# Turning the sample's queries and keys to features over the whole TensorE array, in a hybrid decoder step

## The chip, the cores and the metric

The kernel runs on one core of a Trainium2 chip. The metric is the time of one execution on the device, in microseconds; the median of several runs is taken. The profile is of one execution. Its engines are PE (TensorE: matmuls and transposes), PEld (TensorE's load of the stationary operand), DVE (VectorE), ACT (ScalarE), POOL (GpSimd), and SP, which issues DMAs here.

## The reference, cut to what matters

One inference step of a decoder trunk of two layers, for a prompt of 512 tokens and for a sample group of 8 x 4 = 32 tokens that share all weights. Each layer projects the normalized tokens to ten pieces, mixes them in three groups of heads, and projects back:

```
rq, rk, rv, rg, mq, mk, mv, mg, pu, pg = jnp.split(rmsnorm(x) @ w_in, _split_points(), axis=-1)
# A: retention, 6 heads of 64      (rope; state carried; group norm)
# B: block-sparse attention, 6 heads of 64 (queries and keys normed and roped)
# C: causal pooling over windows 2/4/8/16
mix = concat(r_o * silu(rg), m_o * silu(mg), p_o * silu(pg))
y = x + mix @ w_out
```

The sample's attention reads 2048 earlier positions per sequence through a page table (8 blocks of 256, the best three of them and the own tokens); its retention starts from a given state. Everything is float32. Projections of the prompt are made in three passes of split operands (`F32R`).

## The kernel before, in words

**Tiles.** Tokens lie in 4 tiles of 128 prompt rows and a fifth with the 32 sample rows. A projected query or key tile has tokens on the partitions and 384 features (6 heads of 64) along them. To take scores, it must have features on the partitions, so it is turned by TensorE: three transposes (`tr`, line 360) of 128 features each, against the identity, into a PSUM tile of the ring `tr` (two buffers). For the sample's 32 rows this is done by two functions: `to_blocks` (line 756) for queries, which copies the result to the block layout `qblk` (attention) or a `tabs` buffer (retention), in six small copies, and `to_feat` (line 708) for keys, which copies it to `kTs` in one. In both, a transpose of 32 rows takes a strip of 32 array rows; the kernel calls the mode `ROWS32`. Each is called for two tiles in a layer: eight groups of three transposes in all, 12 of `qk` buffers (queries) and 12 of `ks` buffers (keys).

**Buffers.** A sample's query tile uses one of the three `qk` buffers, a sample's key tile the one `ks` buffer, each 128 x 384; only the first 32 rows are written for the sample. The `qk` buffers serve prompt tiles and residuals in between.

**Modes of the array.** Most matmuls use the whole array (`FULL`). Decode scores and values (`dec`, `pv` in 128x32 forms) divide it by columns, attention values and retention scores in other ways. The planner counts a cost for each change.

**Order.** The order of all instructions on PE, ACT, DVE and POOL is written out by a planner, `_Plan` (line 111 on), when the program is built. Every piece of work is a generator that asks for an engine, keys, buffers and a mode with `R(...)`; the planner starts whichever piece can start first by its estimated times, and adds up an engine's estimated time as instructions are written (`use`, `array`). In `_start`, a piece for PE that isn't of the dense projections counts as due some time after it is ready: `MARGIN` 0.4 us in the undivided mode, `HOLD` 0.6 us if it changes the array away from it, 0.3 or 0.2 us in the other cases. A change of mode costs 0.1 us in the plan, and a transpose 0.06 us for up to 32 rows or 0.1095 us. Work marked "DVE|POOL", as the subtraction for the low half of a weight (`whl`), goes to POOL where DVE's queue is more than 3 us longer. All DMAs of the stretch are issued from SP in the planner's order.

**Start.** `clear` (line 1798) sets constants on POOL, among them `qblk` and `klz`; the first instructions of VectorE turn the first tokens into `XT` (a scaled copy, then a subtraction), and split the first weights (`whl`).

Of the kernel before, what the change touches and what calls it, by code (L numbers as in the profile page):

```python
# [20 lines left out]
NS = 32  # L21
NTOK = SEQ + NS
NB = 8
# [96 lines left out]
class _Plan:  # L120
# [66 lines left out]
        return self.dma_free + 2.8  # L187

    def _start(self, t):
        engines, keys, get, mode = t["want"]  # L190
        at = t["ready"]
        if engines == t.get("engine"):
            at -= self.HOP[engines]
        for k in keys:
            if k not in self.done:
                return None
            at = max(at, self.done[k])
        for name in set(get):
            n = get.count(name)
            r = self.res[name]  # L200
            if len(r) < n:
                return None
            at = max(at, sorted(r)[n - 1])
        best = None
        for e in engines.split("|"):
            s = max(at, self.free[e])
            if e == "SP":
                s = max(s, self.dma_free - 3.0)
            c = s + (self.POOL_LAST if e == "POOL" and "|" in engines else 0.0)
            if e == "PE" and t["prio"][0] < 9:  # L210
                late = self.MARGIN
                if mode != self.mode:
                    late = self.HOLD if self.mode == FULL else 0.3
                elif mode != FULL:
                    late = self.STAY
                c = max(at + late, self.free[e])
            elif e == "PE" and self.mode != FULL:
                c = s + self.LEAVE
            if best is None or c < best[0]:
                best = (c, s, e)  # L220
        c, s, e = best
        return c if e == "PE" else s, s, e
# [30 lines left out]
FULL, COLS32, COLS64, ROWS64, ROWS32 = (128, 128), (128, 32), (128, 64), (64, 128), (32, 128)  # L253


def R(engines, keys=(), get=(), mode=FULL):
    return engines, tuple(keys), tuple(get), mode


class _Timed:  # L260
# [58 lines left out]
def trunk(ctx, tc, depth, xp, xt, xs, xst, kv, sret, spool, pt, nrow, ncol, lpar, w384, w256, cst, y0,  # L319
# [3 lines left out]
    X = _Plan()  # L323
# [23 lines left out]
    def tiles(n):  # L347
        return 32 if n <= 32 else 64 if n <= 64 else 128
# [11 lines left out]
    def tr(out, in_, n):  # L360
        nc.tensor.transpose(out, in_, ident[:n, :n])  # L361
        X.array((tiles(n), 128), 0.1095 if n > 32 else 0.06)
# [344 lines left out]

    def to_feat(src, dst, rows, keys=()):

        yield R("PE", keys, ["tr"], (tiles(rows), 128))  # L710
        p = ps("tr")
        for i in range(3):
            tr(p[:, i * rows:(i + 1) * rows], src[:, i * 128:(i + 1) * 128], rows)
        yield R("ACT|DVE")
        copy(dst(), p[:, :3 * rows].rearrange("p (k n) -> p k n", k=3))
        X.put("tr")

    def feat_tile(L, name, tag, src, t):
# [36 lines left out]

    def to_blocks(src, dst):

        yield R("PE", (), ["tr"], ROWS32)
        p = ps("tr")
        for i in range(3):  # L760
            tr(p[:, i * NS:(i + 1) * NS], src[:, i * 128:(i + 1) * 128], NS)
        yield R("ACT|DVE")
        for i in range(3):
            for h2 in range(2):
                hs = slice(64 * h2, 64 * h2 + 64)
                c0 = (2 * i + h2) * 4
                copy(dst[hs, i, :, c0:c0 + 4], p[hs, i * NS:(i + 1) * NS].rearrange("p (b q) -> p b q", b=NB))
        X.put("tr")

    def head_pick(pv_, out):  # L770
# [43 lines left out]
    def layer(l):  # L814
        ci = l * len(order)
        L = {}
# [172 lines left out]
        def post_mq(t):  # L989
            def f(a):  # L990
                yield R("DVE", [("tabs", l, 0)], ["qk"])
                q_ = buf("qk")
                yield from projected(a, q_, t, L["tabs", 0][:, 0, t], L["tabs", 0][:, 1, t], eps=eps_of(t), norm=norm)
                L["roped", 0] = L.get(("roped", 0), 0) + 1
                if L["roped", 0] == 5:
                    X.put("tabs")
                if t < 4:
                    yield from stacked_tile(L, "qT", q_, t)
                    X.put("qk")
                    X.flag("qT", l, t)  # L1000
                else:
                    L["own"] = [sb([128, HD], "own", 2) for _ in range(2)]
                    L["stat"] = [sb([128, 4, 9], "stat", 2) for _ in range(2)]
                    yield from to_blocks(q_[:NS], qblk)
                    X.put("qk")
                    X.flag("qblk", l)
                    for g in range(2):
                        for n in range(BLOCKS):
                            X.spawn(unit(g, n), 2)
                        X.spawn(combine(g), 1)  # L1010
            return f
# [50 lines left out]
        def post_mk(t):  # L1062
            def f(a):
                tag = "qk" if t < 4 else "ks"
                yield R("DVE", [("tabs", l, 1)], [tag])
                k_ = buf(tag)
                rows = 128 if t < 4 else NS
                yield from projected(a, k_, t, L["tabs", 1][:, 0, t], L["tabs", 1][:, 1, t], eps=eps_of(t), norm=norm)
                L["roped", 1] = L.get(("roped", 1), 0) + 1
                if L["roped", 1] == 5:  # L1070
                    X.put("tabs")
                if t < 4:
                    yield from stacked_tile(L, "kT", k_, t)
                    X.flag("kT", l, t)
                    send(o_kp[l, t * 128:(t + 1) * 128], k_, 196, (), "qk")
                    if t == 0:
                        for qi in range(4):
                            for i in range(3):
                                X.spawn(attention(qi, i), 2)
                else:  # L1080
                    yield R("PE", (), ["kTs"])
                    L["kTs"] = buf("kTs").rearrange("p (i n) -> p i n", i=3)
                    yield from to_feat(k_[:NS], lambda: L["kTs"], NS)
                    X.flag("kTs", l)
                    send(o_ks[l], k_[:NS], 48, (), "ks")
                    X.spawn(own_units(), 1)
            return f
# [190 lines left out]
        def post_rq(t):  # L1278
            def f(a):
                yield R("DVE", (), ["qk"])  # L1280
                q_ = buf("qk")
                rows = 128 if t < 4 else NS
                yield from projected(a, q_, t, cos[:, t], sin[:, t], False if t < 4 else rqs[:rows, t], norm=norm)
                if t < 4:
                    yield from feat_tile(L, "rqT", "qT", q_, t)
                    X.flag("rqT", l, t)
                else:
                    yield R("POOL", (), ["tabs"])
                    rqblk = buf("tabs")
                    G.memset(rqblk, 0.0)  # L1290
                    L["rqblk"] = rqblk.rearrange("p (i b c) -> p i b c", i=3, b=NB)
                    yield from to_blocks(q_[:NS], L["rqblk"])
                    X.flag("rqs", l)
                X.put("qk")
            return f
# [21 lines left out]
        def post_rk(t):  # L1317
            def f(a):
                if t == 0:
                    X.spawn(load_state(), 4)  # L1320
                tag = "qk" if t < 4 else "ks"
                yield R("DVE", (), [tag])
                k_ = buf(tag)
                rows = 128 if t < 4 else NS
                yield from projected(a, k_, t, cos[:, t], sin[:, t], rks[:rows, t] if l or t == 4 else rks0[:, t],
                                     norm=norm)
                if t < 4:
                    yield from feat_tile(L, "rkT", "kT", k_, t)
                    X.spawn(ret_state(t, k_), 0)
                    X.spawn(ret_chunk(t), 2)  # L1330
                else:
                    yield R("PE", (), ["kTs"])
                    L["rkTs"] = buf("kTs").rearrange("p (i n) -> p i n", i=3)
                    yield from to_feat(k_[:NS], lambda: L["rkTs"], NS)
                    X.spawn(ret_sample(), 0)
                    yield R("ACT", (), ["kst"])
                    L["kst"] = buf("kst")
                    yield from stacked(k_[:NS, :384], L["kst"], 2)
                    X.put("ks")
                    X.flag("kst", l)  # L1340
            return f
# [456 lines left out]
    def clear():  # L1798
# [9 lines left out]
        for h2 in range(2):  # L1808
            G.memset(klz[64 - 64 * h2:128 - 64 * h2, h2::2, :].bitcast(F32), 0.0)

    def warm(n):

        yield R("PE", [("ones",)], ["att", "att"])
        o_ = ps("att")[:, 0]
        for _ in range(n):
            mm(o_[:, :128], ones, ones)
            X.use("PE", 0.2)
        X.put("att", 2)
# [96 lines left out]
```

## Time and profile before

| | us |
|---|---|
| median of 3 runs (lowest to highest) | 690.66 (689.52 to 691.14) |
| the profiled execution: its time | 690.34 |
| its span, first to last instruction | 688.6 |
| PE busy in it | 674.9 (98%) |
| DVE busy | 490.4 (71%) |
| ACT busy | 329.8 (48%) |
| POOL busy | 96.9 (14%) |

The span is what the rows of the trace cover; the time has some 1.7 us around it. A matmul's row overlaps the next one's, so PE's busy time is not its work at full rate. The chain of waits follows the work that ended last back to the start, and gives each piece the time from the end of the piece before it to its own end.

### The profile page before, as it was taken

Reading aid. Unit: us, or ns where it says so; the run is one execution under the profiler, and the core shown is the slowest. Engines: PE = TensorE matmul, PEld = TensorE weight load, DVE = VectorE, ACT = ScalarE, POOL = GpSimd, SP = SyncE. Lnnn points to the kernel's source line nnn. Section 1 sums busy time; section 2 is a strip of 40 time slices with the busy share of each in tenths; the row PEclk is TensorE's granted clock in tenths of the full one; section 3 lists DMA queues with packets and bytes.
Section 4 is the critical chain, followed back from the end, with each engine's and each line's share of the span. In section 5 each row is a group of like instructions: output and inputs, shape, how many; then the busy total and the mean of one; then the engine's idle time right before and its main releaser. Section 6 shows DMA issues by size and latency. Waiting matters only on the chain.

```text
span 688.6 us, 17002 instructions
## 1 busy us (share of the span) xinstructions
PE 674.9 (98%) x5958; PEld 570.9 (83%) x5958; DVE 490.4 (71%) x1181; ACT 329.8 (48%) x835; POOL 96.9 (14%) x129
## 2 busy tenths in 40 slices
PE   9998999999999999999999999999999999999997
PEld 8876887777877887999999887877787878889897
DVE  6988887787664469984684789987576545888651
ACT  7562757673342424274464347766432332336620
POOL 2252223000000012300112222230000000132000
PEclk9999999999999999999999999999999999999999
DMA  9947889798989974425744779889979989520462
GB/s 316 323 151 241 272 283 290 248 313 262 313 270 327 321 257 148 127 77 192 242 160 135 226 231 297 262 282 286 307 212 320 308 272 330 181 64 1 135 225 73
DMA packets 111382, 159.76 MB, mean 232 GB/s; under 512 B 13953, under 2 KB 96130, under 8 KB 111298
## 3 DMA queue, kind: packets, MB, share of 16 engines
q1 hardware_dynamic: 110866, 158.42, 71.3%
q8 instruction: 47, 0.77, 0.5%
q10 hardware_dynamic: 432, 0.27, 0.2%
q14 instruction: 37, 0.30, 0.1%
HBM read 148.80 MB, written 9.84 MB: 230 GB/s over the span
## 4 chain that ended last, share of the span: by engine, by line
PE 79%; DVE 13%; POOL 2%; issue 2%; DMA 2%; ACT 2%; ACTq 0%; DVEq 0%; SPq 0%; POOLq 0%
PE acc L351 50%; PE dec L351 10%; PE pv L351 10%; PE tr L361 6%; PE att L351 4%; DVE whl L313 2%; DVE qk L313 1%; POOL gst L313 1%; DVE t L313 1%; POOL qst L313 1%; DVE qT L313 1%; ACT PT L313 1%; DVE bns L313 1%; DMA qk<-y 1%; DVE row L313 1%
## 5 line engine op out<-in xcount | busy, mean ns | idle before, releaser
L351 PE MATMUL acc<-whl,XT 128*128 128x384 f32 (+1 forms) x1680 | 310.6, 337 | 0.8 <-DVE whl L313 0.8
L351 PEld LDWEIGHTS acc<-whl,XT 128*128 128x128 f32 x1680 | 281.0, 189 | 18.4 <-issue 13.5
L351 PE MATMUL acc<-XT,whl 128*128 128x256 f32 (+1 forms) x960 | 138.0, 295 | 1.7 <-DVE qk L313 1.2
L351 PEld LDWEIGHTS acc<-XT,whl 128*128 128x128 f32 x960 | 124.6, 189 | 7.8 <-issue 4.1
L313 DVE TENSOR_TENSOR whl<-wraw,whl 128x768 fp32r<-128x768 f32 (+1 forms) x96 | 87.3, 920 | 13.9 <-ACT whl L313 13.1
L313 ACT CAST whl<-wraw 128x768 fp32r<-128x768 f32 (+1 forms) x100 | 76.5, 783 | 28.9 <-PE acc L351 22.7
L351 PE MATMUL dec<-pk,qblk 128*32 128x256 f32 x768 | 48.1, 383 | 0.0
L313 DVE TENSOR_TENSOR pv<-pv,cst 128x384 f32<-128x384 f32 x40 | 22.4, 561 | 25.2 <-PE pv L351 25.0
L351 PEld LDWEIGHTS dec<-pk,qblk 128*32 128x32 f32 x768 | 22.0, 109 | 17.8 <-issue 4.1
L313 DVE TENSOR_TENSOR mix<-acc,qk 128x384 f32<-128x384 f32 (+1 forms) x24 | 12.3, 511 | 22.9 <-PE acc L351 21.9
L313 ACT ACTIVATE P<-att,ast 128x128 f32<-128x128 f32 (+3 forms) x48 | 25.2, 529 | 6.8 <-DVE ast L313 6.2
L313 POOL TENSOR_TENSOR qst<-qst,mhalf 128x6 f32<-128x6 f32 (+1 forms) x20 | 26.5, 1325 | 1.7
L313 ACT ACTIVATE dPT<-dec 128x256 f32<-128x256 f32 x32 | 12.2, 382 | 29.1 <-PE pv L351 28.9
L313 ACT ACTIVATE t<-acc 128x256 f32<-128x256 f32 (+1 forms) x32 | 12.7, 396 | 27.3 <-PE acc L351 16.1
L313 ACT ACTIVATE dP<-dec,stat 128x256 f32<-128x256 f32 x32 | 15.2, 474 | 20.7 <-DVE stat L313 20.6
L313 POOL TENSOR_SCALAR gst<-gst 128x6 f32<-128x6 f32 (+1 forms) x12 | 4.0, 337 | 137.3 <-DVE gst L313 125.2
L361 PE MATMUL tr<-cst,qk 128*128 128x128 f32 (+1 forms) x108 | 18.4, 280 | 4.7 <-DVE qk L313 4.6
L313 ACT ACTIVATE PT<-PT,gst 128x64 f32<-128x64 f32 x48 | 16.8, 429 | 10.2 <-POOL gst L313 10.2
L361 PEld LDWEIGHTS tr<-cst,qk 128*128 128x128 f32 (+1 forms) x108 | 12.3, 142 | 11.2 <-DVE qk L313 4.7
L313 DVE TENSOR_TENSOR t<-acc,cst 128x192 f32<-128x192 f32 x32 | 9.9, 351 | 16.1 <-PE acc L351 16.1
L313 DVE TENSOR_REDUCE ast<-att 128x2 f32<-128x256 f32 (+3 forms) x24 | 19.8, 825 | 0.8
L313 POOL TENSOR_TENSOR gst<-gst,reps 128x6 f32<-128x6 f32 x4 | 0.9, 221 | 137.1 <-DVE gst L313 137.1
(505 smaller groups left out, 1202.8 us busy)
## 6 DMA issues: line engine op xcount, KB each, us to landing
pk<-kv SPq DMA_DIRECT2D x256, 192.0 KB, 3.8
wraw<-w SPq DMA_DIRECT2D x76, 384.0 KB, 5.2
wraw<-w SPq DMA_DIRECT2D x24, 256.0 KB, 4.1
y<-mix SPq DMA_DIRECT2D x4, 512.0 KB, 3.5
mix<-xt SPq DMA_DIRECT2D x7, 256.0 KB, 5.4
pk<-w SPq DMA_DIRECT2D x4, 384.0 KB, 5.4
o_vp<-tv SPq DMA_DIRECT2D x8, 192.0 KB, 2.3
o_kp<-qk SPq DMA_DIRECT2D x8, 192.0 KB, 4.6
```

Of the source, the lines that this page charges most:

```text
L313: return f(*args, **kw)
L351: nc.tensor.matmul(out, lhsT, rhs, start=start, stop=stop)
L361: nc.tensor.transpose(out, in_, ident[:n, :n])
```

## The change

The three transposes of a sample tile take all 128 rows of its buffer and the whole identity, in mode `FULL`, and write 128 columns each of the PSUM tile; the copies behind them pick the first 32 columns of each 128. So that the rows that no sample token fills hold numbers from the start, `clear` sets the three `qk` buffers and the `ks` buffer to zero on POOL, as its last step, and a key `cleared` is asked for by the transposes in the plan. `R` gets a further argument, `hold`, which `_start` would use in place of `HOLD`. `to_feat` serves the prompt's retention tiles too, with 128 rows; for them nothing but the key is new.

```diff
--- before.py
+++ after.py
@@ -187,7 +187,7 @@
         return self.dma_free + 2.8
 
     def _start(self, t):
-        engines, keys, get, mode = t["want"]
+        engines, keys, get, mode, hold = t["want"]
         at = t["ready"]
         if engines == t.get("engine"):
             at -= self.HOP[engines]
@@ -210,7 +210,7 @@
             if e == "PE" and t["prio"][0] < 9:
                 late = self.MARGIN
                 if mode != self.mode:
-                    late = self.HOLD if self.mode == FULL else 0.3
+                    late = (hold or self.HOLD) if self.mode == FULL else 0.3
                 elif mode != FULL:
                     late = self.STAY
                 c = max(at + late, self.free[e])
@@ -253,8 +253,8 @@
 FULL, COLS32, COLS64, ROWS64, ROWS32 = (128, 128), (128, 32), (128, 64), (64, 128), (32, 128)
 
 
-def R(engines, keys=(), get=(), mode=FULL):
-    return engines, tuple(keys), tuple(get), mode
+def R(engines, keys=(), get=(), mode=FULL, hold=None):
+    return engines, tuple(keys), tuple(get), mode, hold
 
 
 class _Timed:
@@ -707,12 +707,13 @@
 
     def to_feat(src, dst, rows, keys=()):
 
-        yield R("PE", keys, ["tr"], (tiles(rows), 128))
+
+        yield R("PE", [("cleared",), *keys], ["tr"])
         p = ps("tr")
         for i in range(3):
-            tr(p[:, i * rows:(i + 1) * rows], src[:, i * 128:(i + 1) * 128], rows)
+            tr(p[:, i * 128:(i + 1) * 128], src[:, i * 128:(i + 1) * 128], 128)
         yield R("ACT|DVE")
-        copy(dst(), p[:, :3 * rows].rearrange("p (k n) -> p k n", k=3))
+        copy(dst(), p[:, :384].rearrange("p (k n) -> p k n", k=3)[:, :, :rows])
         X.put("tr")
 
     def feat_tile(L, name, tag, src, t):
@@ -755,16 +756,16 @@
 
     def to_blocks(src, dst):
 
-        yield R("PE", (), ["tr"], ROWS32)
+        yield R("PE", [("cleared",)], ["tr"])
         p = ps("tr")
         for i in range(3):
-            tr(p[:, i * NS:(i + 1) * NS], src[:, i * 128:(i + 1) * 128], NS)
+            tr(p[:, i * 128:(i + 1) * 128], src[:, i * 128:(i + 1) * 128], 128)
         yield R("ACT|DVE")
         for i in range(3):
             for h2 in range(2):
                 hs = slice(64 * h2, 64 * h2 + 64)
                 c0 = (2 * i + h2) * 4
-                copy(dst[hs, i, :, c0:c0 + 4], p[hs, i * NS:(i + 1) * NS].rearrange("p (b q) -> p b q", b=NB))
+                copy(dst[hs, i, :, c0:c0 + 4], p[hs, i * 128:i * 128 + NS].rearrange("p (b q) -> p b q", b=NB))
         X.put("tr")
 
     def head_pick(pv_, out):
@@ -1001,7 +1002,7 @@
                 else:
                     L["own"] = [sb([128, HD], "own", 2) for _ in range(2)]
                     L["stat"] = [sb([128, 4, 9], "stat", 2) for _ in range(2)]
-                    yield from to_blocks(q_[:NS], qblk)
+                    yield from to_blocks(q_, qblk)
                     X.put("qk")
                     X.flag("qblk", l)
                     for g in range(2):
@@ -1080,7 +1081,7 @@
                 else:
                     yield R("PE", (), ["kTs"])
                     L["kTs"] = buf("kTs").rearrange("p (i n) -> p i n", i=3)
-                    yield from to_feat(k_[:NS], lambda: L["kTs"], NS)
+                    yield from to_feat(k_, lambda: L["kTs"], NS)
                     X.flag("kTs", l)
                     send(o_ks[l], k_[:NS], 48, (), "ks")
                     X.spawn(own_units(), 1)
@@ -1289,7 +1290,7 @@
                     rqblk = buf("tabs")
                     G.memset(rqblk, 0.0)
                     L["rqblk"] = rqblk.rearrange("p (i b c) -> p i b c", i=3, b=NB)
-                    yield from to_blocks(q_[:NS], L["rqblk"])
+                    yield from to_blocks(q_, L["rqblk"])
                     X.flag("rqs", l)
                 X.put("qk")
             return f
@@ -1331,7 +1332,7 @@
                 else:
                     yield R("PE", (), ["kTs"])
                     L["rkTs"] = buf("kTs").rearrange("p (i n) -> p i n", i=3)
-                    yield from to_feat(k_[:NS], lambda: L["rkTs"], NS)
+                    yield from to_feat(k_, lambda: L["rkTs"], NS)
                     X.spawn(ret_sample(), 0)
                     yield R("ACT", (), ["kst"])
                     L["kst"] = buf("kst")
@@ -1808,6 +1809,12 @@
         for h2 in range(2):
             G.memset(klz[64 - 64 * h2:128 - 64 * h2, h2::2, :].bitcast(F32), 0.0)
 
+        yield R("POOL", (), ["ks"] + ["qk"] * RES["qk"])
+        for tag in ["ks"] + ["qk"] * RES["qk"]:
+            G.memset(buf(tag), 0.0)
+            X.put(tag)
+        X.flag("cleared")
+
     def warm(n):
 
         yield R("PE", [("ones",)], ["att", "att"])
```

## Rows read from the trace of the kernel before

**Rows 1.** The page's fourth part: shares of the chain that ended last.
```profile
PE 79%; DVE 13%; POOL 2%; issue 2%; DMA 2%; ACT 2%; ACTq 0%; DVEq 0%; SPq 0%; POOLq 0%
```

**Rows 2.** Chain of waits, first 30 us (start, us, what); shares of 29 to 45 us.
```profile
5.94 0.42 DVE XT L313 x2
...
8.00 7.27 PE acc L351 x40
...
by line: POOL qst L313 39.6%; DVE qk L313 12.2%; issue 9.6%; DVE qT L313 9.6%; DVE t L313 7.3%; DVE qst L313 5.9%; POOL rs L313 5.5%; DVE kT L313 4.8%; DVE acc L313 3.5%; DVE stat L313 2.6%; DVE psc L313 1.5%; DVE rs L313 1.1%; DVE gnw L313
```

**Rows 3.** Chain of waits, 50 to 63 us; last row PE's timeline with its wait.
```profile
50.20 2.51 DVE whl L313
...
58.76 4.33 PE acc L351 x18
...
57.86 0.90 PE L361 MATMUL tr<-cst,qk 128*128 128x128 f32 x3 [2.40 <-DVE qk L313]
```

**Rows 4.** Instructions of line 361: ns minimum, median, maximum; first and last start; forms.
```profile
L361 PE MATMUL tr<-cst,qk x108: 221/272/476, 37.6 to 604.6; 128*128 128x128 f32 x96, 32*128 32x32 f32 x12
...
L361 PE MATMUL tr<-cst,ks x12: 221/222/246, 77.3 to 564.0; 32*128 32x32 f32 x12
```

**Rows 5.** Chain of waits at three groups of narrow transposes.
```profile
157.80 0.89 PE tr L361 x7
...
375.81 0.30 PE tr L361 x3
376.10 2.30 PE acc L351 x12
...
509.85 1.80 PE acc L351 x12
```

**Rows 6.** Chain of waits at undivided transposes and the work beside them.
```profile
402.19 0.48 PE tr L361 x3
...
407.64 3.17 PE acc L351 x18
410.81 0.33 PE tr L361 x3
...
411.14 2.11 PE acc L351 x12
...
438.77 1.59 PE acc L351 x12
```

**Rows 7.** Timeline of POOL at the start (start, us, instruction, idle before).
```profile
1.59 0.77 POOL L313 MEMSET Sst<- 128x384 f32 x2
2.42 2.80 POOL L313 MEMSET klz<- 64x1536 f32 x2
20.04 1.17 POOL L313 TENSOR_TENSOR rs<-rs,mhalf 128x1 f32<-128x1 f32 x1 [14.82 <-DVE rs L313]
```

**Rows 8.** Timeline of VectorE at the start.
```profile
4.86 0.51 DVE L313 TENSOR_SCALAR XT<-mix,ncol 128x256 fp32r<-128x256 f32 x1 [4.86 <-DMA ncol<-ncol]
5.94 0.35 DVE L313 TENSOR_SCALAR XT<-mix,ncol 128x256 fp32r<-128x256 f32 x1 [0.57 <-DMA mix<-xt]
```

**Rows 9.** Timelines of VectorE and POOL, 48 to 52 us and 112 to 115 us.
```profile
48.78 0.96 DVE L313 TENSOR_TENSOR whl<-wraw,whl 128x768 fp32r<-128x768 f32 x1
...
50.12 2.59 DVE L313 TENSOR_TENSOR whl<-wraw,whl 128x768 fp32r<-128x768 f32 x1
...
49.90 1.99 POOL L313 TENSOR_TENSOR whl<-wraw,whl 128x768 fp32r<-128x768 f32 x1 [1.12 <-ACT whl L313]
...
112.95 0.72 DVE L313 TENSOR_SCALAR P<-P,ast 128x256 f32<-128x256 f32 x1
...
112.20 1.31 POOL L313 TENSOR_TENSOR s<-tabs 128x676 f32<-128x676 f32 x1
113.59 1.31 POOL L313 TENSOR_TENSOR tabs<-s 128x672 f32<-128x672 f32 x1
```

**Rows 10.** Table of stretches: busy time of engines, granted clock, DMA share, GB/s.
```profile
58.00:60.00 2.00, 2.00 (x8) 2.00 (x9) 1.24 (x4) 1.17 (x3) 0.00 (x0) 0.50 0.86 267
```

## Prediction

> **What bounds the kernel now.** I read the page's head first. The profiled execution took 690.34 us with a span of 688.6 us; the runs' median is 690.66, so what is summed against the profiled execution gets 0.32 us added at the end. The chain of work that ended last is 79% TensorE and 13% VectorE [rows 1]. An average hides stages, so I read the chain in order of time next. Its start belongs to VectorE: the token load lands, VectorE makes `XT` of it from 5.94 us, and its subtraction for `whl` releases TensorE at 8.00 [rows 2]. From about 22 to 91 us the chain belongs mostly to VectorE, and to the roots on POOL that VectorE waits for: the shares of the stretch from 29 to 45 us show what that looks like, with no TensorE piece among them [rows 2]. In that stretch TensorE waits 2.40 us in one piece, behind a VectorE subtraction that took 2.59 us [rows 3, 9]. From 91 us on the chain is nearly all TensorE. So a microsecond saved on TensorE counts after 91 us, and one lost on VectorE counts before.
>
> **The transposes.** There are 12 narrow transposes of `qk` tiles and 12 of `ks` tiles, 32x128 in and 32x32 of identity [rows 4]: eight groups of three. What one group costs in its place is read from the chain of waits, where a piece lasts from one end to the next. Between undivided work the narrow group takes 0.30 us and the 12 matmuls behind it 2.30 [rows 5]; three undivided transposes take 0.33 and the same 12 matmuls, with the same follower, 2.11 [rows 6]. So the transposes themselves get 0.03 dearer, and the return to the undivided array, 0.19, goes: 0.16 us saved.
>
> Now the eight places, each as it stands today:
> - 37.64 and 77.28 us, where both sorts begin [rows 4]: in the VectorE stretch, off the chain. Saved 0.16 each, worth nothing; the cover is the wait at 57.86 and the VectorE chain to 91 us.
> - 375.81 [rows 5], and 220.47 and 415.94 which are like it (undivided work on both sides): 0.16 each, together -0.48.
> - 509.55 comes right behind decode matmuls, which leave the array divided anyway. Today 0.30, as at 375.81, and 1.80 for the 12 matmuls behind [rows 5]; an undivided group behind divided work takes 0.48, and 12 matmuls of that form 1.59 [rows 6]: 2.10 against 2.07, -0.03. At 157.80, also behind decode work, seven transposes take 0.89 together [rows 5]; undivided 0.48 + 4 x 0.11 = 0.92 (0.11 is a third of 0.33): +0.03.
> - 563.91 is followed by divided work, so the change of mode only comes later and no return is saved: 0.33 for 0.30, +0.03.
>
> The sum is -0.45 us. The bounds: all six on the chain at 0.19 give -1.14; if no place saves anything and each pays 0.03, +0.18. I keep -0.45 because each place has its own rows. Copies out of PSUM keep their number and elements, only strided: nothing in the rows prices a stride, and two of the eight groups lie off the chain; their readers (`qblk`, `kTs`, the table) begin decode units, for which TensorE has other work at all six places, so I take zero.
>
> A page of the Trainium skill speaks against the change. The row first: a narrow group takes 0.30 and an undivided one 0.33 [rows 5, 6], though the identity that it goes through has 128 columns and not 32 [rows 4]. If time went by columns, an undivided group would take 4 x 0.30 = 1.20, and six on the chain 6 x 0.90 = 5.4 us more. The skill's "TensorEngine Tiling (Array Packing)", sections "Theoretical Speedup" and "Tiling Modes", gives up to 4x for a dimension of 32 or less, and a drain at each change of mode; by its factor, too, the sum would be about +5.4 instead of -0.45. The rows bear out the drain and not the factor.
>
> **The memsets.** Four memsets of 128x384 join POOL's queue at the end of `clear`. Two of that size took 0.77 us together today [rows 7], so four take about 1.55 us, and they follow `klz`, which ends at 2.42 + 2.80 = 5.22: they run from about 5.2 to 6.8. On POOL nothing is queued behind them until 20.04 [rows 7], and the cleared buffers are first wanted by the joins of the sample's projections, ahead of the first transpose at 37.64 [rows 4]: the decode and dense work between covers them. No DMA is moved and SP's queue is untouched. But VectorE is working then, on the chain [rows 2]. Its first `XT` instruction, while `klz` is being cleared, took 0.51 us and ended at 5.37, 0.15 behind the memset; the second took 0.35 with POOL idle [rows 8]. The same pattern stands later: a VectorE scaling issued at 112.95 took 0.72 and ended 0.16 after POOL's instruction of 112.20 + 1.31, and POOL's next one at 113.59 didn't keep it out [rows 9]. So the second `XT` instruction, at 5.94, falls among the memsets and may wait for one of them to end: nothing if it falls between two, at most one memset, 0.39, since it gets in before the next. The two-input instructions behind it might wait for another 0.39: no row shows one beside a memset. Bounds 0 to 0.8; I take 0.2, the middle of the first wait alone. It goes in full down the chain: `whl`, the start of TensorE at 8.00 and all behind it.
>
> The skill's "SBUF — State Buffer", section on the two physically separate sides, says why: the port pair of VectorE and GpSimd is an exclusive lock, but an instruction with two SBUF inputs meets it only against a GpSimd instruction that reads SBUF, which a memset doesn't. By that the upper end would be 0.4, not 0.8; no row before the change shows it.
>
> **The order.** `_Plan` writes out the whole order from estimated times. Three of its inputs move: a narrow group out of an undivided array is held 0.6 (`HOLD`), an undivided one 0.4 (`MARGIN`); it costs 3 x 0.06 + 2 x 0.1 = 0.38 in the plan's terms today and 3 x 0.1095 = 0.33 then; and the plan's own VectorE times shift with the memsets. (`hold` itself changes nothing: no call of the diff gives it.) The first group lies at 37.64 us, so everything behind may be placed differently: other pieces between the same neighbours, other choices of POOL or VectorE. That has no row. Its size is bounded by what a misplaced piece costs today. At 50.12 the subtraction on VectorE took 2.59, its like at 48.78 took 0.96, because POOL held a `whl` subtraction from 49.90 for 1.99 [rows 9]: 1.63 on the chain. The wait that follows, 2.40 [rows 3], is followed by a clock at half speed, 1.2 instead of 2.4 GHz, through 58 to 60 us and beyond [rows 10]: three transposes and 18 matmuls took 0.90 + 4.33 on the chain [rows 3] where 0.33 + 3.17 is usual (410.81 and 407.64 [rows 6]): 1.73. So one such misplacement weighs up to 3.4 us, either way.
>
> **Sum.** -0.45 + 0.2 = -0.25: 690.34 becomes 690.1 in the profiled execution, and 690.4 against the median.
>
> **Rivals.**
> - The order loses today's misplacement. For it: it stands at 50 us, behind the first moved group and behind the shifted start, and rests on a `whl` half given to POOL 0.2 us before VectorE began its own. Against it: VectorE is overfull in that stretch in any order. Gone in full it gives 690.4 - 3.4 = 687.0; the lock alone, 688.8.
> - The order keeps it and gains another: a second `whl` half put on POOL while VectorE has one to do too, in the stretch up to 91 us where VectorE is the chain. One lock of 1.63 gives 692.0; if TensorE's wait behind it costs the clock as today's did, 690.4 + 3.4 = 693.8. It decides from the first such lock on the chain; after 91 us VectorE has slack and the same lock costs nothing.
> - Undivided transposes are dear after all, and time goes by columns: 690.4 + 0.45 + 5.4 = 696.2. The 0.33 speaks against it. (This is the packing page's factor.)
> - Nothing of it reaches the end: the order between is the same and the gain and the start cancel, 690.3 to 690.7. This is the edge of my forecast and not told apart from it.
>
> **How the numbers follow.** 0.2% of this kernel, 1.38 us, is about what a measurement can tell from no change. My forecast (with the last rival) has 0.40 and lies within it: its own range is -1.14 + 0 to +0.18 + 0.8, 689.5 to 691.6. The lost misplacement has 0.34, the new one 0.24, the dear transposes 0.02. So faster 0.34, the same 0.40, slower 0.26. The range leaves about 0.1 at either side: the full 3.4 gain and a little more, 686.8, and the new lock with half of the clock's loss, 692.0 + 0.8 = 692.8.
>
> **What would show it.** In the trace after: 24 transposes of 128x128 more and no 32x32 ones with identity; chain pieces of 0.33 at the places between undivided work, and the 12 matmuls behind at 2.11; four memsets at 5.2 to 6.8 us, VectorE's second `XT` instruction at 0.35 to 0.75, and TensorE's third group starting at 8.0 to 8.4 rather than 8.00; the 2.59 us subtraction and the 2.40 us wait present or gone. I am wrong if the order changes little and the time still moves by over 1.4 us, if transposes over 128 rows take much more than 0.33 in three, or if the two-input instructions behind the second `XT` one are held and push the start by more than 0.8.

## The result, and the profile after

The changed kernel takes 695.47 us (median of 6 runs, 695.20 to 696.34) against 690.90 (689.52 to 692.45) for the kernel before: a ratio of 1.0074, 95% interval 1.0060 to 1.0088. It is slower by 4.6 us; I had forecast no change (690.4), and 695.47 lies above my range of 686.8 to 692.8 too. The profiled execution took 695.46 us.

The page after: span, busy times, shares of the chain, and the group of weight halves (`whl`) that POOL subtracts (count, busy time and mean, idle time before).

```profile
span 693.7 us, 17016 instructions
...
PE 676.1 (97%) x5958; PEld 571.4 (82%) x5958; DVE 485.8 (70%) x1170; ACT 334.1 (48%) x842; POOL 111.8 (16%) x137
...
PE 81%; DVE 13%; ACT 2%; issue 2%; POOL 1%; DMA 1%; ACTq 0%; DVEq 0%; POOLq 0%
...
L313 POOL TENSOR_TENSOR whl<-wraw,whl 128x768 fp32r<-128x768 f32 (+1 forms) x9 | 17.3, 1917 | 61.4 <-ACT whl L313 36.8
```

The shares hardly differ from [rows 1]. The span grew by 5.1 us: TensorE is busy for 1.2 us more (674.9 to 676.1) and idle for 3.9 us more (693.7 - 676.1 = 17.6, against 688.6 - 674.9 = 13.7). POOL does nine halves where it did four.

What the diff itself touches went nearly as costed. First the view of line 361, then the chain (its first two rows are the landing of the tokens and VectorE's `XT` behind it), then VectorE's and POOL's timelines at the start and TensorE's third group there:

```profile
L361 PE MATMUL tr<-cst,qk x108: 270/272/331, 35.1 to 608.5; 128*128 128x128 f32 x108
L361 PE MATMUL tr<-cst,ks x12: 270/271/272, 73.5 to 576.9; 128*128 128x128 f32 x12
...
1.64 4.14 DMA mix<-xt
...
5.80 0.51 DVE XT L313 x2
...
73.71 0.33 PE tr L361 x3
...
376.31 0.52 PE tr L361 x3
376.83 2.11 PE acc L351 x12
...
4.71 1.54 DVE L313 TENSOR_SCALAR XT<-mix,ncol 128x256 fp32r<-128x256 f32 x2 [4.71 <-DMA ncol<-ncol]
6.16 0.86 DVE L313 SCALAR_TENSOR_TENSOR XT<-mix,ncol,XT 128x256 fp32r<-128x256 f32 x2
...
5.17 0.42 POOL L313 MEMSET ks<- 128x384 f32 x1
5.53 1.42 POOL L313 MEMSET qk<- 128x384 f32 x3
...
7.95 2.37 PE L351 MATMUL acc<-whl,XT 128*128 128x384 f32 x12 [0.25 <-DVE whl L313]
```

The transposes of `qk` and `ks` tiles are all 128x128 now. The group of three at 73.71 takes 0.33 us, and the 12 matmuls behind the one at 376.31 take 2.11 where they took 2.30 [rows 5]. That group itself stands behind 0.06 us of "issue", and its 0.52 is dearer than either price in [rows 6]. The memsets run from 5.2 to 6.95. TensorE's third group starts at 7.95, not later than in [rows 2], but the tokens landed 0.13 us earlier too: it starts 2.17 us behind their landing at 5.78, where the kernel before took 2.09 (its tokens landed at 1.63 + 4.28 = 5.91).

The loss shows in what TensorE waits for. Its waits after 91 us, by what ended them (total us, times, longest; the five largest of ten):

```profile
PE tr L361 <- DVE so L313: 2.0, 1, 2.0
PE tr L361 <- ACT P L313: 2.0, 2, 1.3
PE tr L361 <- DVE qk L313: 1.8, 2, 1.1
PE acc L351 <- DVE t L313: 0.4, 1, 0.4
PE acc L351 <- DVE whl L313: 0.4, 1, 0.4
```

The rows of this view add up to 7.9 us after 91 us; before, they add up to 5.1, and neither `so` nor `P` of ScalarE is among them.

Most of the loss lies in one stretch. At two later points TensorE has started the same set of instructions in both kernels: the first 3294 of 5958 by 388.03 us before and 389.62 after, and the first 5523 by 626.40 and 632.22. What lies between, in the table of stretches (window, length, busy time of PE, PEld, DVE, ACT, POOL, granted clock, DMA share, GB/s), before and after:

```profile
388.03:626.40 238.37, 237.44 (x2230) 192.95 (x2230) 176.20 (x443) 112.93 (x307) 31.90 (x40) 1.00 0.78 251
...
389.62:632.22 242.60, 238.69 (x2230) 193.53 (x2230) 171.00 (x440) 118.63 (x323) 35.84 (x41) 1.00 0.76 246
```

Up to there the changed kernel is 1.6 us behind. In this stretch it loses another 4.2: TensorE is idle for 3.91 us instead of 0.93, with waits of 0.68 at 404.75, 0.74 at 501.41 and 2.04 at 608.29, and busy for 1.25 us more. In the rest it gets 0.7 back.

Timelines of POOL, VectorE and TensorE at the two stretches behind the largest waits:

```profile
146.21 1.98 POOL L313 TENSOR_TENSOR whl<-wraw,whl 128x768 fp32r<-128x768 f32 x1 [3.63 <-ACT whl L313]
148.13 0.74 POOL L313 MEMSET tabs<- 128x768 f32 x1
...
144.24 0.49 DVE L313 TENSOR_SCALAR P<-P,ast 128x512 f32<-128x512 f32 x1
...
146.41 2.74 DVE L313 TENSOR_SCALAR P<-P,ast 128x512 f32<-128x512 f32 x1
...
152.93 0.65 PE L361 MATMUL tr<-cst,P 128*128 128x128 f32 x4 [1.25 <-ACT P L313]
...
608.06 0.18 DVE L313 TENSOR_TENSOR so<-dec,cst 128x32 f32<-128x32 f32 x1
...
608.29 0.52 PE L361 MATMUL tr<-cst,qk 128*128 128x128 f32 x3 [2.04 <-DVE so L313]
```

At 146 us a POOL half stands beside a VectorE scaling, which takes 2.74 us where its like takes 0.49: it ends at 149.15, behind the half (148.19) and the memset that follows it on POOL (148.87). The softmax behind it is late, and TensorE waits. The kernel before has no POOL half between 49.90 and 266.59 us. At 608 us TensorE waits for VectorE, whose rows mark no wait from 594.83 to 611 us.

In the stretch of [rows 9] and [rows 10], the lock has not gone; it has changed its victim:

```profile
51.22 2.58 POOL L313 TENSOR_TENSOR whl<-wraw,whl 128x768 fp32r<-128x768 f32 x1
...
52.04 2.17 DVE L313 TENSOR_TENSOR qk<-qk,qst 128x384 f32<-128x384 f32 x1
54.14 0.95 DVE L313 TENSOR_TENSOR whl<-wraw,whl 128x768 fp32r<-128x768 f32 x1
...
59.38 0.52 PE L361 MATMUL tr<-cst,qk 128*128 128x128 f32 x3 [1.20 <-ACT dP L313]
...
58.00:60.00 2.00, 0.80 (x7) 0.65 (x6) 1.96 (x5) 0.99 (x5) 0.57 (x1) 1.00 0.80 251
```

The 2.17 us instruction is a product on a query tile; its like at 58.69 takes 0.55. TensorE's wait here is now 1.20 and not 2.40, and the granted clock of 58 to 60 us is 1.00 and not 0.50.

### The profile page after: what moved, and what is told of

Its sections match the earlier page's. It is cut to its first block, busy times and chain, and to the rows that moved or that the text cites. A ratio compares the mean times of both kernels' runs of the same rounds, so it can differ in the third digit from the quotient of the medians.

```text
span 693.7 us, 17016 instructions
## 1 busy us (share of the span) xinstructions
PE 676.1 (97%) x5958; PEld 571.4 (82%) x5958; DVE 485.8 (70%) x1170; ACT 334.1 (48%) x842; POOL 111.8 (16%) x137
## 4 chain that ended last, share of the span: by engine, by line
PE 81%; DVE 13%; ACT 2%; issue 2%; POOL 1%; DMA 1%; ACTq 0%; DVEq 0%; POOLq 0%
PE acc L351 51%; PE dec L351 10%; PE pv L351 10%; PE tr L361 6%; PE att L351 4%; DVE qk L313 2%; DVE whl L313 1%; DVE t L313 1%; DVE row L313 1%; DVE comb L313 1%; POOL gst L313 1%; DVE P L313 1%; ACT PT L313 1%; DVE acc L313 1%; DVE On L313 1%
## 5 line engine op out<-in xcount | busy, mean ns | idle before, releaser
L351 PE MATMUL acc<-XT,whl 128*128 128x256 f32 (+1 forms) x960 | 139.6, 294 | 0.4 <-DVE t L313 0.4
L313 ACT CAST whl<-wraw 128x768 fp32r<-128x768 f32 (+1 forms) x100 | 76.7, 783 | 30.6 <-PE acc L351 24.2
L313 DVE TENSOR_TENSOR whl<-wraw,whl 128x768 fp32r<-128x768 f32 (+1 forms) x91 | 80.1, 894 | 15.4 <-ACT whl L313 14.6
L313 DVE TENSOR_TENSOR pv<-pv,cst 128x384 f32<-128x384 f32 x40 | 22.4, 560 | 17.6 <-PE pv L351 17.3
L313 ACT ACTIVATE P<-att,ast 128x128 f32<-128x128 f32 (+3 forms) x48 | 25.2, 529 | 7.3 <-DVE ast L313 7.2
L313 DVE TENSOR_TENSOR mix<-acc,qk 128x384 f32<-128x384 f32 (+1 forms) x24 | 12.2, 510 | 23.2 <-PE acc L351 22.2
L313 POOL TENSOR_TENSOR whl<-wraw,whl 128x768 fp32r<-128x768 f32 (+1 forms) x9 | 17.3, 1917 | 61.4 <-ACT whl L313 36.8
L313 POOL TENSOR_TENSOR qst<-qst,mhalf 128x6 f32<-128x6 f32 (+1 forms) x20 | 26.5, 1326 | 1.7
L361 PE MATMUL tr<-cst,qk 128*128 128x128 f32 x108 | 18.7, 282 | 6.0 <-DVE qk L313 2.7
L313 DVE TENSOR_REDUCE stat<-dec 128x1 f32<-128x256 f32 x32 | 13.5, 420 | 15.6 <-PE dec L351 15.4
L361 PEld LDWEIGHTS tr<-cst,qk 128*128 128x128 f32 x108 | 12.3, 141 | 12.9 <-issue 6.8
L313 POOL TENSOR_SCALAR gst<-gst 128x6 f32<-128x6 f32 (+1 forms) x12 | 4.1, 338 | 116.8 <-DVE comb L313 116.6
L313 ACT ACTIVATE PT<-PT,gst 128x64 f32<-128x64 f32 x48 | 16.8, 428 | 12.5 <-POOL gst L313 12.5
L313 ACT ACTIVATE t<-acc 128x256 f32<-128x256 f32 (+1 forms) x32 | 12.6, 393 | 20.1 <-DVE acc L313 13.5
L361 PEld LDWEIGHTS tr<-cst,P 128*128 128x128 f32 x120 | 14.0, 142 | 9.7 <-issue 4.3
L361 PE MATMUL tr<-cst,P 128*128 128x128 f32 x120 | 19.9, 280 | 2.0 <-ACT P L313 2.0
L313 ACT COPY PT<-tr 128x256 f32<-128x256 f32 (+3 forms) x41 | 16.0, 413 | 11.8 <-PE tr L361 11.7
```

The source lines that it names most:

```text
L313: return f(*args, **kw)
L351: nc.tensor.matmul(out, lhsT, rhs, start=start, stop=stop)
```

## The experiments

Each was timed beside the kernel before; "ratio" is against that, with its 95% interval. It differs by up to 0.0014 from the quotient of the two medians.

**The transposes and memsets in the old order.** The diff's operations in the order of the kernel before: the plan is told the old costs. In the traces, TensorE, ScalarE and VectorE have the same instructions in the same order as before; POOL has the four memsets more.

```diff
+    def wide(out, in_, n):
+        nc.tensor.transpose(out, in_, ident)
+        X.array((tiles(n), 128), 0.1095 if n > 32 else 0.06)
...
+        for tag in ["ks"] + ["qk"] * RES["qk"]:
+            nc.gpsimd.memset(buf(tag), 0.0)
```

> The transposes over 128 rows and the four memsets in the order that the kernel before has, instruction for instruction: the plan is not told of either. If the order that the plan writes is what costs the 4.6 us, this runs at about 690.9 - 0.25 = 690.6 us, ratio 0.998 to 1.001. If the transposes or the memsets themselves are dear, it runs like the changed kernel, about 695.5 us, ratio near 1.007.

691.59 us, ratio 1.0000 (0.9989 to 1.0011). The chain of this kernel between undivided work, and behind decode work:

```profile
376.68 0.33 PE tr L365 x3
377.01 2.10 PE acc L351 x12
...
510.28 0.48 PE tr L365 x3
510.75 1.59 PE acc L351 x12
```

The prices of my sum are met: 0.33 + 2.10 for 0.30 + 2.30, and 0.48 + 1.59 as forecast behind divided work. At the places of 157.80, 220.47 and 563.91 the chain of this run has 0.48 + 0.44, 0.33 + 2.11 and 0.33, also as forecast; at that of 415.94 it does not pass through TensorE. The sum of -0.25 lies within the interval (0.76 us either way). So the operations cost nothing beyond that interval.

**The new order without the transposes.** The changed kernel with the narrow transposes back, told to the plan as undivided. Its trace has the order of the changed kernel on all four engines.

```diff
+    def narrow(out, in_):
+        nc.tensor.transpose(out, in_, ident[:NS, :NS])
+        X.array(FULL, 0.1095)
```

> The mirror: the changed kernel's order and memsets, but the sample's transposes take 32 rows again. If the order is the cause, it stays slow: 695.5 us plus up to 0.9 for changing the array's mode eight times, about 695.9, ratio 1.006 to 1.010. If the transposes over 128 rows are the cause, it falls back to about 691 us, ratio near 1.000.

696.73 us, 1.0073 (1.0055 to 1.0090): the whole loss without an undivided transpose. The order carries it.

**Which input of the plan.** The memsets alone, known to the plan; and the undivided transposes with memsets unknown to it (`G.` tells the plan of an operation, `nc.gpsimd.` doesn't).

```diff
-            G.memset(buf(tag), 0.0)
+            nc.gpsimd.memset(buf(tag), 0.0)
```

> The kernel before with the four memsets known to the plan; the transposes stay narrow. The order differs from before's from about 20 us on. If the memsets, by moving the plan's VectorE times, bring the bad order, about 695 us, ratio 1.005 to 1.009. If the mode of the transposes brings it, 690 to 692 us, ratio 0.998 to 1.002.

> The changed kernel with the four memsets hidden from the plan, so that only the mode, the hold and the cost of the transposes move the order. If these bring the bad order, about 695 us, ratio 1.005 to 1.009. If the memsets' place in the plan does, 690 to 692 us, ratio 0.998 to 1.002.

Memsets alone: 693.27 us, 1.0038 (1.0021 to 1.0056). Transposes alone: 695.75, 1.0060 (1.0040 to 1.0080). Either input is enough for a slower order.

**Other orders by small changes of the plan's constants**, in the kernel before (`HOLD` 0.55 or 0.65), and in the changed one: the sample's transposes due 0.6 us after they are ready, as the narrow ones were; `HOLD` 0.65; `MARGIN` 0.45.

```diff
-    HOLD = 0.6
+    HOLD = 0.55
```

> The kernel before with one constant of the plan moved, HOLD 0.55 for 0.6: the same work, other places. Theory A, the lottery: any rewriting of the order moves the time by some tenths of a per cent and mostly up, ratio 0.999 to 1.010. Theory B, undivided transposes planned too early are what hurts: with narrow transposes the order hardly matters, ratio 0.998 to 1.002.

> The same with HOLD 0.65. Theory A: ratio 0.999 to 1.010, not tied to the size of the change. Theory B: 0.998 to 1.002.

> The changed kernel, but in the plan a sample's transposes count as due 0.6 us after they are ready, as they did before, and not 0.4. Theory B: the earlier due time is the cause, so this goes back to 691 us, ratio 0.998 to 1.002. Theory A: it is another draw, anywhere from 690 to 697 us.

> The changed kernel with HOLD 0.65, which touches no transpose of the sample any more. Theory A: another draw, 690 to 697 us, as likely below the changed kernel's 695.5 as above. Theory B: stays at 695 to 696 us.

> The changed kernel with MARGIN 0.45 for 0.4: one more order for the same work. Theory A, the lottery: 691 to 698 us. If the changed kernel's order were unusually bad, most others would be faster, 691 to 694.

| kernel | us | ratio, interval |
|---|---|---|
| before, `HOLD` 0.55 | 698.02 | 1.0092 (1.0072 to 1.0113) |
| before, `HOLD` 0.65 | 694.03 | 1.0045 (1.0029 to 1.0062) |
| after, due 0.6 | 694.36 | 1.0047 (1.0029 to 1.0065) |
| after, `HOLD` 0.65 | 697.81 | 1.0093 (1.0065 to 1.0121) |
| after, `MARGIN` 0.45 | 700.73 | 1.0140 (1.0116 to 1.0164) |

All are slower than the kernel before, with narrow transposes or undivided ones. They are not independent draws: some orders share long parts. That of the transposes alone, for one, has TensorE's last 4666 of 5958 instructions as the changed kernel has them. That the transposes come too early because they are due after 0.4 and not 0.6 us doesn't explain it: with 0.6 about two thirds of the loss stay. The traces of the two slowest hold one long wait, and a clock of half speed behind it: first `HOLD` 0.55 (TensorE's timeline, a stretch), then `MARGIN` 0.45. The profiled execution of the first took 702.47 us, 4.4 more than its median, that of the second 702.40, 1.7 more:

```profile
302.59 0.40 PE L361 MATMUL tr<-cst,row 128*64 128x128 f32 x1 [3.49 <-DVE row L313]
...
304.00:306.00 2.00, 2.00 (x8) 1.79 (x6) 1.97 (x7) 1.13 (x2) 0.00 (x0) 0.50 0.00 0
```

```profile
617.81 0.42 PE L361 MATMUL tr<-cst,row 128*64 128x128 f32 x1 [3.36 <-DVE row L313]
...
618.00:620.00 2.00, 2.00 (x11) 2.00 (x11) 1.96 (x7) 0.00 (x0) 0.00 (x0) 0.50 0.00 0
```

**The 2.04 us wait, by moving the waiting piece.** The changed kernel, with the last prompt tile's retention keys in the second layer due 2.5 us later.

```diff
-                    yield from feat_tile(L, "rkT", "kT", k_, t)
+                    yield from feat_tile(L, "rkT", "kT", k_, t, 2.5 if l and t == 3 else None)
```

> The changed kernel with one piece of the plan moved: the last prompt tile's retention keys of the second layer are turned 2.5 us later in the plan, so that the three transposes for which TensorE waits 2.04 us at 608.29 come behind six dense and twelve decode matmuls. The order is the same up to there. If that wait is part of the loss, its 2.04 us shrinks by what is put before it (about 1 to 1.6 us), and the time falls to 694.0 to 694.8, ratio 1.005 to 1.007. If waits there are made good by the stage behind, which waits for VectorE and POOL anyway, no change: 695.5, 1.007 or more.

697.28 us, 1.0098 (1.0070 to 1.0126): no gain, but no test of what that wait is worth either, for TensorE's timeline shows the same wait before another piece:

```profile
609.29 0.28 PE L361 MATMUL tr<-cst,so 128*32 128x128 f32 x1 [2.05 <-DVE so L313]
```

VectorE's queue is late, not one piece badly placed on TensorE.

**The old lock.** The kernel before, and the old order with undivided transposes and memsets, with POOL's half of 49.90 us [rows 9] done by VectorE in its place.

```diff
+                    if X.engine == "POOL" and not moved:
+                        moved.append(ci)
+                        X.use("POOL", 0.153 + W2 * 0.0021)
+                        nc.vector.tensor_tensor(out=hl[:, 1, :W2], in0=raws[ci, s_][:, :W2],
+                                                in1=hl[:, 0, :W2].bitcast(F32), op=OP.subtract)
...
```

> The kernel before with one instruction moved: the low half of a weight that POOL subtracts at 49.90 us is subtracted by VectorE, in the place that the plan gave to POOL. By the prediction's step, the lock costs 1.63 us on the chain and the clock behind the wait 1.73; VectorE's own subtraction costs 0.96 there. So 690.9 - 0.67 = 690.2 if the clock still falls, and 688.5 if it no longer does; ratio 0.996 to 0.9995. If the waits are made good later, 1.000.

> The same move with the transposes over 128 rows and the memsets in the old order. It should stand to the run without them (old_no_lock) as the change's own worth: -0.25 by the prediction's sum, so 688.2 to 690.0, ratio 0.996 to 0.9995. This is the version that could beat both kernels.

688.95 us, 0.9974 (0.9960 to 0.9988), and 689.24, 0.9981 (0.9965 to 0.9996). Timelines of VectorE and TensorE, a piece of the chain, and the stretch of [rows 10], in the first:

```profile
50.04 0.95 DVE L313 TENSOR_TENSOR whl<-wraw,whl 128x768 fp32r<-128x768 f32 x1
...
53.20 0.96 DVE L479 TENSOR_TENSOR whl<-wraw,whl 128x768 fp32r<-128x768 f32 x1
...
57.01 0.55 PE L361 MATMUL tr<-cst,qk 128*128 128x128 f32 x3 [1.63 <-DVE qk L313]
...
57.56 3.17 PE acc L351 x18
...
58.00:60.00 2.00, 2.00 (x13) 2.00 (x12) 1.40 (x4) 1.86 (x7) 0.00 (x0) 1.00 0.96 276
```

The 2.59 us instruction takes 0.95, and the clock stays up. The rival's mechanism was real: VectorE gains 1.63 and pays 0.96 for the half, 0.67 less. TensorE's three transposes and 18 matmuls take 0.55 + 3.17 for 0.90 + 4.33 [rows 3], so the clock's part is 1.51 of the 1.73 that I had. Together that is 2.2 by the rows, and 2.0 by the medians.

**POOL's halves in both orders.** VectorE does some of POOL's halves in their places; the order is the same else.

```diff
+                    if X.engine == "POOL":
+                        pooled.append(ci)
+                        if len(pooled) in (3, 4, 6, 7):
+                            G.eng = nc.vector
                     add2(hl[:, 1, :W2], raws[ci, s_][:, :W2], hl[:, 0, :W2].bitcast(F32), OP.subtract)
+                    G.eng = nc.gpsimd
```

> The changed kernel with only the four halves of 140.76, 146.21, 485.73 and 491.37 us issued on VectorE, in their places; the kernel before has no POOL subtraction of a weight in these stretches. Lock theory: the locks at 146.41 (2.25 us) and 491.40 (2.17 us) go against four halves of 0.88; the waits of TensorE at 152.93 (1.25) and 501.41 (0.74) shrink, and the layer stages return 1 to 2 us: 693.3 to 694.5. Order theory: no change, 695 to 696.

> The changed kernel with only the two halves of 599.56 and 601.95 us issued on VectorE, in their places, ahead of the 2.04 us wait for VectorE at 608.29. Lock theory: the instructions beside them on VectorE at 599.93 to 603 lose 0.5 us or so, and two halves cost it 1.76, so this one would be no gain: 695 to 697. Order theory: the wait grows by the 0.9 to 1.8 us: 696 to 697.5. It tells whether VectorE is really the bound there: if the time does not rise, the wait at 608.29 is not on the path that sets the end.

> The changed kernel with all nine weight halves that POOL subtracts in it issued on VectorE instead, in the places that the plan gave them; all other work and its order are the same. Lock theory: in the changed kernel VectorE instructions beside such a POOL subtraction are stretched: 2.17 us for 0.56 at 52.04, 2.74 for 0.49 at 146.41, 1.86 for 0.56 at 268.50, 2.55 for two of 0.19 at 491.40, together 1.61 + 2.25 + 1.30 + 2.17 = 7.3 us of VectorE, and TensorE waits for what stands behind. Without them VectorE pays about 0.88 for each half: much of the 5 us comes back, 690.5 to 693. Order theory: the loss lies in the order as a whole, VectorE pays 9 x 0.88 = 7.9 us where it is late anyway: 694.5 to 697.

> The changed kernel with its first seven POOL halves (51.22 to 491.37 us) on VectorE in their places; the two of 599.56 and 601.95 stay on POOL, since moving them alone cost 4 us. If the costs add: 1.0083 for all nine less 1.0132 - 1.0074 for the last two gives 1.0025, 692.8; the four in the middle gave 1.0045, so the first, the 128x512 one and that of 268.11 would be worth another 1.4 us. Order theory, with the four in the middle as the whole share of the locks: 694.5.

> The kernel before with all four halves that POOL subtracts in it (49.90, 266.59, 422.97, 602.03 us) issued on VectorE in their places. The first of them alone gave 688.95, 2.0 us less. Lock theory: the one at 266.59 costs VectorE a stretched instruction as at 268.50 in the changed kernel; the rest is near even: 688 to 689.5. Order theory: the same as the first alone or slower by the halves where VectorE is late (602): 689 to 690.5. If this and the changed kernel without POOL halves end within 1 us of each other, the locks carry the difference; if 4 to 5 us stay between them, they carry none of it.

> Undivided transposes and the four memsets in the order of the kernel before, and all four POOL halves on VectorE: the change without its order, on the best version so far (688.14, 0.9952). My step of -0.45 and at most 0.2 at the start, if nothing else moves: 687.9, no difference that can be measured; had the undivided transposes a cost that the order hid, 689.5 or more.

| halves moved to VectorE | us | ratio, interval |
|---|---|---|
| after: four in the middle | 694.57 | 1.0045 (1.0028 to 1.0061) |
| after: the last two | 700.44 | 1.0132 (1.0111 to 1.0153) |
| after: all nine | 697.13 | 1.0083 (1.0059 to 1.0107) |
| after: all but the last two | 693.94 | 1.0052 (1.0036 to 1.0069) |
| before: all four | 688.14 | 0.9952 (0.9934 to 0.9970) |
| old order, undivided, memsets: all four | 689.00 | 0.9981 (0.9965 to 0.9996) |

The four in the middle are worth 1 to 2 us: 2.0 by the ratios (1.0074 - 1.0045 = 0.0029, of 691; the intervals just touch), 0.9 by the medians of the two sessions (695.47 - 694.57). The lock at 146 us is gone, and the wait behind it shrinks, as the timelines of VectorE and TensorE in that kernel show:

```profile
147.41 0.48 DVE L313 TENSOR_SCALAR P<-P,ast 128x512 f32<-128x512 f32 x1
...
152.37 0.66 PE L361 MATMUL tr<-cst,P 128*128 128x128 f32 x4 [0.37 <-ACT P L313]
```

The other three give nothing more. The last two are to be kept on POOL: moved, VectorE is later still at 608 us, and the clock falls. TensorE's timeline and a stretch of the run with the last two moved:

```profile
608.47 0.85 PE L361 MATMUL tr<-cst,qk 128*128 128x128 f32 x3 [2.37 <-DVE so L313]
...
612.00:614.00 2.00, 2.00 (x12) 2.00 (x11) 1.55 (x2) 0.36 (x2) 1.52 (x2) 0.50 0.64 179
```

So that wait lies on the path that sets the end. But the locks don't carry the difference between the orders: moving POOL's halves gains 3.3 us of the old order too (0.9952), and the best edits of each end 0.93% apart (1.0045 and 0.9952). With no half on POOL at all the two orders lie 9.0 us apart (697.13 and 688.14), further than the 4 to 5 us at which I had said that the locks carry none of it. The undivided transposes show no gain on that version either; 0.9981 beside 0.9952 may even be a loss, but the intervals overlap.

## Why the prediction was wrong

- **The transposes (-0.45)**: right at the five places that the chain of the old order shows; too small to be seen in the time. The rival that they are dear fell with 0.33.
- **The memsets (+0.2, bounds 0 to 0.8)**: right in kind, small in size. VectorE's scalings lie among them (4.71 to 6.25 for two), and the chain's `XT` piece there takes 0.51 us for 0.42 [rows 2]; the two-input instructions take 0.86 for two, as before the change (0.87), and aren't held, so nothing of the upper bound comes of it: from the tokens' landing to TensorE's third group it takes 0.08 us longer. The Trainium skill, "SBUF — State Buffer", section "Who interferes with whom", says that a VectorE instruction with two SBUF inputs contends with a GpSimd instruction that reads SBUF, not with one that only writes it. The 0.86 agrees with that.
- **The order**: this step failed. I gave it no term in the likeliest case, sized it in the rivals as "one such misplacement" of up to 3.4 us "either way", and gave the good side more chance (0.34) than the bad (0.24). The runs showed eight distinct new orders (the changed kernel's, the memsets' alone, the transposes' alone, and the five of the constants' table), all slower, by 0.4 to 1.4%; new_late_608, the changed kernel's order with one late piece, is slower too. Among these orders of one planner that of the kernel before is the best, by 0.38% or more, so a new draw had one likely side. Nor is the loss one misplacement of 3.4 us at most: it is 1.6 us up to 388 us and 4.2 in the stretch behind, in several waits.
- **The rival "loses today's misplacement"**: its price was about right (1.63 and 1.51 in old_no_lock, for 1.63 and 1.73), but it didn't happen so. POOL's half moved to 51.22 and locked another instruction for 2.17 us. Only the clock's part came back.
- **The rival "gains another lock"**: the mechanism came true, in the wrong place. I confined it to the time before 91 us, since "after 91 us VectorE has slack and the same lock costs nothing". The POOL halves at 140 to 147 and 485 to 493 us carry 1 to 2 of the 5 us that the ratio gives. The slack was read from the chain of one order, and too freely even there. "Nearly all TensorE" from 91 us on leaves out three stretches of the kernel before in which the chain is off TensorE: 259.2 to 293.7, 597.7 to 607.1 (with `604.19 0.94 DVE whl L313`, a weight half on VectorE, among its pieces) and 613.9 to 637.2 us. In the changed kernel three more such stretches come up, 144.8 to 152.9, 396.5 to 404.8 and 488.0 to 501.4 us, mostly of VectorE. The second of the old ones grows to 593.3 to 615.2 and the third shrinks to 638.1 to 642.5, so their lengths alone are not the loss.
- **What stays open**: the rest, 0.45%, some 3 us. The wait of 2.04 us at 608 us is part of it by the run with the last two halves moved, but no run took it away. The 1.25 us of added busy time between 389.62 and 632.22 us isn't explained: the granted clock is 1.00 there in both kernels. Whether the order before was picked for its time, no run shows.

## What to carry to other kernels

Where a planner writes the whole order, any change of its inputs is two changes: the operation, and a new draw of the order. Time the operation alone with the old order kept (here 1.0000), and the order alone without the operation (here 1.0073), before you credit either; and try several orders, for here they lay up to 1.4% apart while the operation alone wasn't told from nothing (0.11% either way). Of an order that is the best of its neighbours, expect a redraw to lose. Before you call an engine slack in a stage, look for its pieces in the chain of that very stage.

The lowest time here has the old order with POOL's four weight halves on VectorE: 688.14 us, 0.9952.

## What was unexpected on the chip

- Work that moves from POOL to a fuller VectorE can gain: a half costs VectorE 0.95 us, and beside one on POOL VectorE's instructions took 1.6 us (52.04) and 2.25 us (146.41) longer than their like.
- The granted clock fell to 0.50 (1.2 GHz) behind waits of 2.37, 2.40, 3.36 and 3.49 us, and stayed at 1.00 (2.4 GHz) behind those of 1.63 us (58 to 60 us in old_no_lock) and 2.04 us (608 to 610 us after). In the run with the last two halves moved this wait was 0.33 us longer than after (2.37 for 2.04), the clock stayed at 0.50 from 610 to 618 us, and the time is 4 us longer (1.0132 - 1.0074).
